# Last feed-forward stage: gate and up products of seventeen pairs as seven 256-column block products, with a hand-written order on every engine

## Chip, core and metric

The kernel runs on one core of a Trainium2 chip. The metric is the device time of one execution in microseconds (us), as the median over several runs. Matmuls run on TensorE (PE in the profile, its weight loads as PEld), elementwise work on VectorE (DVE) and ScalarE (ACT); GpSimd (POOL) and SyncE (SP) issue DMAs here.

## What is computed

A trunk of two layers on 512 tokens of width 1024 in float32. Each layer is half a feed-forward block, a mixer (Mamba-2 in layer 0, a diagonal state-space model "S5" in layer 1), and half a feed-forward block; an RMS norm ends the trunk.

```python
def rmsnorm(x, g):
    xf = x * lax.rsqrt(jnp.mean(x * x, axis=-1, keepdims=True) + NORM_EPS)
    return xf * g

def swiglu(h, w_in, w_out):                 # w_in 1024 x 5632, w_out 2816 x 1024
    gate, up = jnp.split(h @ w_in, 2, axis=-1)
    return (jax.nn.silu(gate) * up) @ w_out

for i in range(2):
    x = x + 0.5 * swiglu(rmsnorm(x, ffn1_norm[i]), ffn1_w_in[i], ffn1_w_out[i])
    x = x + mixer_i(rmsnorm(x, mix_norm[i]))
    x = x + 0.5 * swiglu(rmsnorm(x, ffn2_norm[i]), ffn2_w_in[i], ffn2_w_out[i])
return rmsnorm(x, final_norm)
```

## The kernel before

The residual stream stands transposed in SBUF as eight tiles `xT[d]` of 128 channels by 512 tokens. The stages run one after another: f1_0, ssd, f2_0, f1_1, s5, f2_1. The change concerns f2_1, the last, which ends in the final norm.

**Products in two parts.** Every matmul operand is split into a float32r value and a float32r remainder (`H` and `L` of the tokens, `hi` and `lo` of the weights). `proj` forms hi·H + hi·L + lo·H: three matmuls (lines 227, 228 and 229) for each 128-row slice of the contraction, each with its own 128x128 weight load and 512 moving columns. A weight tile goes through `fetch_w` (line 209, a DMA from the SP queue into `wst`), then `split_w`: a cast on ACT (line 218) and a subtraction on DVE (line 220).

**One feed-forward stage** (`ffn`). The 2816 hidden channels are 22 pairs: a gate tile and an up tile of 128 channels. A pair costs two projections of 24 matmuls each. Then DVE multiplies both by the norm's factor `rbc` (lines 259 and 262), ACT takes the silu (260), DVE multiplies (263), ACT casts (`ah`, 265) and DVE subtracts (`al`, 267). The pairs come in parts of 8, 7 and 7 (`PARTS`). After each part comes its share of the output projection: eight tiles `po`, each added to `xT[d]` by DVE (274). After the last part the new `xT[d]` goes to the final norm: ACT squares it (171) and scales it (`xg`, 1093), PE transposes it (1098), and DVE copies the result out (1099). `Prep.flush` issues the transposes of tile d when tile d+1 has been projected.

The norm's gain is multiplied into the tokens beforehand, but its factor `rbc` only reaches the result after the projection, so that the matmuls need not wait for the sum of squares. That sum is formed on PE (line 148) and `newton_rsqrt` on DVE, then spread by four transposes (157) and copied by ACT (204).

**What sets the order.** In this stage a scheduler orders all engines. In the trace each engine runs its instructions in the order in which they stand, so that one with an unmet wait holds all that stand behind it on its engine.

Of the kernel before, what the change touches and what calls it, by code (L numbers as in the profile page):

```python
# [9 lines left out]
F32 = mybir.dt.float32  # L10
F32R = mybir.dt.float32r
I32 = mybir.dt.int32
AF = mybir.ActivationFunctionType
OP = mybir.AluOpType
AX = mybir.AxisListType

T = 512
D = 1024
KD = 8
FF = 2816  # L20
FT = 22
# [4 lines left out]
MAN = {mybir.EngineType.PE}  # L26
# [4 lines left out]
def trunk_kernel(ctx, tc, x, ffn1_norm, ffn1_w_in, ffn1_w_out, mix_norm, ffn2_norm, ffn2_w_in, ffn2_w_out,  # L31
# [3 lines left out]
    nc = tc.nc  # L35
    V, S, G, PE = nc.vector, nc.scalar, nc.gpsimd, nc.tensor
# [3 lines left out]
    hpool = ctx.enter_context(tc.tile_pool(name="hpool", bufs=8))  # L40
    work = ctx.enter_context(tc.tile_pool(name="work", bufs=2))
# [3 lines left out]
    def mm_ps():  # L45
        return psum.tile([128, 512], F32, tag="mm", name="mm", bufs=4)

    def aux_ps():
        return psum.tile([128, 512], F32, tag="aux", name="aux", bufs=4)
# [23 lines left out]
    xT = [const.tile([128, T], F32, name=f"xT{d}") for d in range(KD)]  # L73
# [44 lines left out]
    def col(nm, j=0, n=1):  # L118
        i, r0 = C[nm]
        return cols[i][:, r0 + j:r0 + j + n]  # L120
# [32 lines left out]
    def bcast_rows(y4):  # L153

        p = aux_ps()
        for c in range(4):
            PE.transpose(p[:, c * 128:(c + 1) * 128], y4[:, c:c + 1].to_broadcast([128, 128]), ident)
        return p

    class Prep:  # L160


        def __init__(self, kind, gain, sink=None):
            self.kind, self.gain, self.sink = kind, gain, sink
            self.H, self.L = [None] * KD, [None] * KD
            self.acc = None
            self.later = []
# [25 lines left out]
        def sums(self):  # L193
            self.ps = compact_sum([self.acc, self.sq])
# [5 lines left out]
        def finish(self):  # L200
            self.y4 = newton_rsqrt(self.ps[:, 0:4], 4, 1.0 / D)
            if self.kind == "hilo":
                self.rbc = work.tile([128, T], F32, name="rbc")
                S.copy(self.rbc, bcast_rows(self.y4))


    def fetch_w(src, kt, eng=None):
        st = wpool.tile([128, KD, 128], F32, name="wst", bufs=4)[:, :kt]
        i = (eng or nc.sync).dma_start(st, src.rearrange("(k p) c -> p k c", p=128))
        return st, i  # L210

    def load_w(src, kt, eng=None):

        return split_w(fetch_w(src, kt, eng)[0], kt)

    def split_w(st, kt):
        hi = wpool.tile([128, KD, 128], F32R, name="whi", bufs=3)[:, :kt]
        S.copy(hi, st)  # L218
        lo = wpool.tile([128, KD, 128], F32R, name="wlo", bufs=3)[:, :kt]
        V.tensor_tensor(lo, st, hi.bitcast(F32), op=OP.subtract)  # L220
        return hi, lo

    def proj(ps, w, H, L, first=True, last=True):
        hi, lo = w
        n = len(H)
        for k in range(n):
            PE.matmul(ps, hi[:, k], H[k], start=first and k == 0, stop=False)  # L227
            PE.matmul(ps, hi[:, k], L[k], start=False, stop=False)  # L228
            PE.matmul(ps, lo[:, k], H[k], start=False, stop=last and k == n - 1)  # L229


    def ffn(pr, w_in, w_out, nxt, fill=(), ready=(), done=(), pad=0):

        fill, ready, done = list(fill), list(ready), list(done)

        def pop():
            if fill:
                fill.pop(0)()

        with tc.tile_pool(name="ffn", bufs=2) as fp:  # L240
            if pad:
                fp.tile([128, pad // 4], F32, name="pad", bufs=1)
            for a, b in PARTS:
                AH, AL = [], []
                for f in range(a, b):
                    if done:
                        pg, pu = done.pop(0)
                    else:
                        pg, pu = mm_ps(), mm_ps()
                        wg = ready.pop(0) if ready else load_w(w_in[:, f * 128:(f + 1) * 128], KD)  # L250
                        proj(pg, wg, pr.H, pr.L)
                        if f == 0:
                            pr.sums()
                        wu = ready.pop(0) if ready else load_w(w_in[:, FF + f * 128:FF + (f + 1) * 128], KD)
                        proj(pu, wu, pr.H, pr.L)
                        if f == 0:
                            pr.finish()
                    gt = fp.tile([128, T], F32, name="gt")
                    V.tensor_tensor(gt, pg, pr.rbc, op=OP.mult)  # L259
                    S.activation(gt, gt, AF.Silu)  # L260
                    up = fp.tile([128, T], F32, name="up")
                    V.tensor_tensor(up, pu, pr.rbc, op=OP.mult)  # L262
                    V.tensor_tensor(up, up, gt, op=OP.mult)  # L263
                    ah = fp.tile([128, T], F32R, name="ah", bufs=8)
                    S.copy(ah, up)  # L265
                    al = fp.tile([128, T], F32R, name="al", bufs=8)
                    V.tensor_tensor(al, up, ah.bitcast(F32), op=OP.subtract)  # L267
                    AH.append(ah)
                    AL.append(al)
                    pop()  # L270
                for d in range(KD):
                    po = mm_ps()
                    proj(po, load_w(w_out[a * 128:b * 128, d * 128:(d + 1) * 128], b - a), AH, AL)
                    V.scalar_tensor_tensor(xT[d], po, 0.5, xT[d], op0=OP.mult, op1=OP.add)  # L274
                    if b == FT:
                        nxt.flush()
                        nxt.take(d)
                    pop()
            while fill:
                fill.pop(0)()  # L280
        nxt.flush()
        if nxt.kind != "hilo":
            nxt.sums()
            nxt.finish()


    def ssd(pr, nxt):
# [295 lines left out]
    s5 = {}  # L583
# [503 lines left out]
    fin = {}  # L1087
# [17 lines left out]

    def prep_for(st):
        if st is None:
            fin["p"] = ctx.enter_context(tc.tile_pool(name="fin", bufs=2))
            return Prep("final", ("fin", 0), fin_sink)
        if st == "ssd":  # L1110
            return Prep("hilo", ("mix", 0))
        if st == "s5":
            s5["op"] = op_es.enter_context(tc.tile_pool(name="s5op", bufs=2))
            s5["up"] = up_es.enter_context(tc.tile_pool(name="s5u", bufs=2))
            return Prep("s5", ("mix", 8), s5_sink)
        L = int(st[-1])
        return Prep("hilo", (st[:2], 8 * L))
# [22 lines left out]
    with tc.manual_schedule(engines={mybir.EngineType.Activation, mybir.EngineType.DVE, mybir.EngineType.PE}):  # L1140
        xps, w = {}, {}
# [13 lines left out]
        def part(i, j, k, n=1):  # L1155
            proj(done[i][j], [w_[:, k:k + n] for w_ in w[2 * i + j]], prep.H[k:k + n], prep.L[k:k + n], first=k == 0,
                 last=k + n == KD)
# [52 lines left out]
    if "s5" in stages:  # L1210
        before = [s for s in stages[:stages.index("s5")] if s[0] == "f"]
        s5_pre = before[-3:-1]
    for i, s in enumerate(stages[:-1]):
        pr, prep = prep, prep_for(stages[i + 1])
        nxt = prep
        if s == "ssd":
            with tc.manual_schedule(engines=MAN):
                ssd(pr, nxt)
        elif s == "s5":
            with tc.manual_schedule(engines=MAN):  # L1220
                s5_stage(pr, nxt)
            op_es.close()
        else:
            L = int(s[-1])
            wi, wo = (ffn1_w_in, ffn1_w_out) if s[:2] == "f1" else (ffn2_w_in, ffn2_w_out)
            if s in s5_pre[:1]:
                ffn(pr, wi[L], wo[L], nxt, fill=pre0, ready=ready, done=done, pad=224)
                pre_es.close()
            elif s in s5_pre:
                with tc.tile_pool(name="pre1", bufs=2) as pp:  # L1230
                    ffn(pr, wi[L], wo[L], nxt, fill=s5_setup(pp, 1))
            elif stages[i + 1] == "s5":
                fill = [lambda: None] * 46
                for j in range(2):
                    for h in range(2):
                        fill[24 + 4 * h + 2 * j] = lambda j=j, h=h: out_ops(j, h)
                for j in range(2):
                    fill[40 + 2 * j] = lambda j=j: in_ops(j)
                fill[44] = lambda: out_ops(2, 0)
                for j in range(2 * NR):  # L1240
                    fill[39 + 2 * j] = lambda j=j: res_w(j)
                ffn(pr, wi[L], wo[L], nxt, fill=fill)
                up_es.close()
            else:
                ffn(pr, wi[L], wo[L], nxt)
    for t in range(4):
        if t % 2:
            V.tensor_scalar(fin["o"][:, t], fin["o"][:, t], prep.y4[:, t:t + 1], None, op0=OP.mult)
# [32 lines left out]
```

## Time and profile before

| | us |
|---|---|
| median of 3 runs (2090.33 to 2095.71) | 2092.37 |
| the profiled execution's own time | 2093.88 |
| its span | 2092.1 |
| last stage within the span: first matmul with its weights, end of the span | 1712.56, 2092.1 |
| PE busy, DVE busy, ACT busy over the span | 2035.6, 1250.0, 788.9 |

The span is the time that the profile covers; 1.8 us of the execution lie around it. All times in rows are counted from the span's start.

### The profile page before, as it was taken

Reading aid. Unit: us, or ns where it says so; the run is one execution under the profiler, and the core shown is the slowest. Engines: PE = TensorE matmul, PEld = TensorE weight load, DVE = VectorE, ACT = ScalarE, POOL = GpSimd, SP = SyncE. Lnnn points to the kernel's source line nnn. Section 1 sums busy time; section 2 is a strip of 40 time slices with the busy share of each in tenths; the row PEclk is TensorE's granted clock in tenths of the full one; section 3 lists DMA queues with packets and bytes.
Section 4 is the critical chain, followed back from the end, with each engine's and each line's share of the span. In section 5 each row is a group of like instructions: output and inputs, shape, how many; then the busy total and the mean of one; then the engine's idle time right before and its main releaser. Section 6 shows DMA issues by size and latency. Waiting matters only on the chain.

```text
span 2092.1 us, 26974 instructions
## 1 busy us (share of the span) xinstructions
PE 2035.6 (97%) x10675; PEld 1677.9 (80%) x10675; DVE 1250.0 (60%) x2119; ACT 788.9 (38%) x1140; POOL 84.6 (4%) x144
## 2 busy tenths in 40 slices
PE   8999999999999999999999999999996999999997
PEld 6788888878878877887788888888886888888886
DVE  6699445678875777557854554343458545444444
ACT  5223323556653574333423332232354333222223
POOL 1000000021110110000000000000011000000000
PEclk9999999999999999999999999999997999999999
DMA  7654432433333324435553353333367233333321
GB/s 163 136 160 142 148 100 83 111 116 105 101 108 114 107 64 125 144 113 162 145 145 89 102 193 91 102 94 104 91 191 235 62 90 101 101 94 88 110 84 58
DMA packets 411519, 244.29 MB, mean 117 GB/s; under 512 B 44952, under 2 KB 396864, under 8 KB 411136
## 3 DMA queue, kind: packets, MB, share of 16 engines
q1 hardware_dynamic: 381968, 203.19, 34.5%
q0 software_dynamic: 7984, 25.46, 3.7%
q10 hardware_dynamic: 21440, 13.91, 2.3%
q8 instruction: 84, 1.38, 0.3%
q14 instruction: 43, 0.35, 0.1%
HBM read 217.74 MB, written 24.25 MB: 116 GB/s over the span
## 4 chain that ended last, share of the span: by engine, by line
PE 59%; DVE 2%; ACT 1%; issue 1%; DVEq 0%; ACTq 0%
PE mm L227 19%; PE mm L228 19%; PE mm L229 19%; DVE z L1001 0%; PE aux L229 0%; PE aux L228 0%; PE aux L227 0%; PE aux L861 0%; PE aux L1019 0%; PE aux L867 0%; PE aux L992 0%; DVE z L997 0%; DVE z L999 0%; DVE z L998 0%; ACT z L1006 0%
## 5 line engine op out<-in xcount | busy, mean ns | idle before, releaser
L218 ACT CAST whi<-wst 128x1024 fp32r<-128x1024 f32 (+2 forms) x357 | 361.3, 1013 | 945.2 <-PE mm L228 662.8
L227 PE MATMUL mm<-hH,whi 128*128 128x512 f32 x1800 | 708.7, 394 | 5.8 <-ACT whi L218 4.1
L228 PE MATMUL mm<-hL,whi 128*128 128x512 f32 x1800 | 704.1, 391 | 0.0
L229 PE MATMUL mm<-hH,wlo 128*128 128x512 f32 x1800 | 703.2, 391 | 0.5 <-DVE wlo L220 0.5
L220 DVE TENSOR_TENSOR wlo<-wst,whi 128x1024 fp32r<-128x1024 f32 (+2 forms) x357 | 418.4, 1173 | 86.7 <-ACT whi L218 83.4
L227 PEld LDWEIGHTS mm<-hH,whi 128*128 128x128 f32 x1800 | 339.3, 189 | 77.6 <-ACT whi L218 4.5
L229 PEld LDWEIGHTS mm<-hH,wlo 128*128 128x128 f32 x1800 | 339.1, 188 | 72.6 <-DVE wlo L220 1.0
L228 PEld LDWEIGHTS mm<-hL,whi 128*128 128x128 f32 x1800 | 339.3, 189 | 69.6 <-issue 0.6
L228 PE MATMUL mm<-al,whi 128*128 128x512 f32 x704 | 274.5, 390 | 0.0
L229 PE MATMUL mm<-ah,wlo 128*128 128x512 f32 x704 | 274.2, 390 | 0.0
L227 PE MATMUL mm<-ah,whi 128*128 128x512 f32 x704 | 273.5, 390 | 0.0
L262 DVE TENSOR_TENSOR up<-mm,rbc 128x512 f32<-128x512 f32 x88 | 60.7, 690 | 213.4 <-PE mm L229 213.3
L274 DVE SCALAR_TENSOR_TENSOR xT<-mm,xT 128x512 f32<-128x512 f32 x96 | 66.0, 689 | 188.4 <-PE mm L229 188.3
L228 PEld LDWEIGHTS mm<-al,whi 128*128 128x128 f32 x704 | 132.2, 188 | 28.0 <-issue 0.6
L227 PEld LDWEIGHTS mm<-ah,whi 128*128 128x128 f32 x704 | 132.2, 188 | 27.5 <-issue 0.4
L229 PEld LDWEIGHTS mm<-ah,wlo 128*128 128x128 f32 x704 | 132.2, 188 | 27.3 <-issue 0.2
L259 DVE TENSOR_TENSOR gt<-mm,rbc 128x512 f32<-128x512 f32 x88 | 60.6, 689 | 149.7 <-PE mm L229 146.4
L384 DVE SCALAR_TENSOR_TENSOR cv<-raw,cols,cv 128x512 f32<-128x512 f32 x96 | 76.1, 803 | 7.0 <-ACT cv L382 6.4
L265 ACT CAST ah<-up 128x512 fp32r<-128x512 f32 x88 | 54.9, 624 | 65.7 <-DVE up L263 65.2
L263 DVE TENSOR_TENSOR up<-up,gt 128x512 f32<-128x512 f32 x88 | 60.7, 690 | 7.1 <-ACT whi L218 0.5
L267 DVE TENSOR_TENSOR al<-up,ah 128x512 fp32r<-128x512 f32 x88 | 60.0, 683 | 0.8 <-ACT ah L265 0.7
L260 ACT ACTIVATE gt<-gt 128x512 f32<-128x512 f32 x88 | 55.0, 627 | 13.7 <-DVE gt L259 8.5
(325 smaller groups left out, 1704.2 us busy)
## 6 DMA issues: line engine op xcount, KB each, us to landing
wst<-in_ffn_w_in_dram SPq DMA_DIRECT2D x176, 512.0 KB, 3.9
wst<-in_ffn_w_out_dram SPq DMA_DIRECT2D x64, 448.0 KB, 3.7
wst<-in_ssd_in_proj_dram SPq DMA_DIRECT2D x48, 512.0 KB, 4.0
wst<-in_ffn_w_out_dram SPq DMA_DIRECT2D x32, 512.0 KB, 4.0
dec<-d_cs POOLq DMA_DIRECT2D x16, 512.0 KB, 4.2
opP<-d_P SPq DMA_DIRECT2D x16, 512.0 KB, 5.4
wst<-in_s_glu_w_dram POOLq DMA_DIRECT2D x12, 512.0 KB, 5.3
d_t<-p_cs POOLq DMA_DIRECT2D x8, 512.0 KB, 4.2
```

The source lines that it names most:

```text
L218: S.copy(hi, st)
L220: V.tensor_tensor(lo, st, hi.bitcast(F32), op=OP.subtract)
L227: PE.matmul(ps, hi[:, k], H[k], start=first and k == 0, stop=False)
L228: PE.matmul(ps, hi[:, k], L[k], start=False, stop=False)
L229: PE.matmul(ps, lo[:, k], H[k], start=False, stop=last and k == n - 1)
L259: V.tensor_tensor(gt, pg, pr.rbc, op=OP.mult)
L260: S.activation(gt, gt, AF.Silu)
L262: V.tensor_tensor(up, pu, pr.rbc, op=OP.mult)
L263: V.tensor_tensor(up, up, gt, op=OP.mult)
L267: V.tensor_tensor(al, up, ah.bitcast(F32), op=OP.subtract)
L274: V.scalar_tensor_tensor(xT[d], po, 0.5, xT[d], op0=OP.mult, op1=OP.add)
L384: V.scalar_tensor_tensor(cv, raw[:, 1 + j:T + 1 + j], col("cw", j * 32 + ct), cv, op0=OP.mult, op1=OP.add)
```

## The change

`ffn7` takes the place of `ffn` in the last stage. Pairs 0 to 4 are computed as before. Meanwhile `build` forms the tokens after the norm (gain and `rbc` multiplied in) for the pairs 5 to 21.

For those, a pair is seen as a product of 2x2 blocks: gate and up tile, two halves of the contraction, two halves of 256 tokens. Seven block products, each of four 128-row slices, take the place of eight. `mul` issues one: 12 matmuls of 256 columns (lines 368 to 370). A pair has 84 of these where it had 48 of 512 columns. The sums that such a scheme needs are made in three places:

- of tokens, once: `build` makes seven blocks (`th` and `tl`, four slices each) from `n` and `t`;
- of weights, per pair: with `g` and `u` the gate and the up weights in two halves, `five` is u0+u1 (DVE, into PSUM), `six` is five+g0 (DVE), `add7` is u0+g0 and `add3` is six+g1 (both by an accumulating DMA from the POOL queue, 256 KB). `four` splits each of them on ACT (line 395) and DVE (398);
- of results: a product is accumulated in PSUM tiles `A`, `B` and `E`, and copied out (ACT lines 440, 480 and 499) between products that go on accumulating in `A`.

`iteration` writes the order of all engines down by hand. While PE works on pair `P`, DVE and ACT prepare the weights of the next, `N`, and finish the one before, `prev`. The seven products stand on PE in this order: W1 and (for `prev`) W3, W2, (for `prev`) W4, then W6, W7, W5. The pairs now come in parts of 5, 4, 4, 4 and 5. In a part with a `prev` left over, the first three tiles of the output projection are computed without its last pair and completed afterwards (`part`).

```diff
@@ class Prep, finish
-                self.rbc = work.tile([128, T], F32, name="rbc")
+                self.rbc = work.tile([128, T], F32, name="rbc", bufs=1)
@@ after ffn
+    def accumulate(dst, src):
+        G.dma_start(dst, src, accum_op=OP.add)
...
+    def ffn7(pr, w_in, w_out, nxt, parts, fill=(), late=None):
...
+        sv = es7.enter_context(tc.tile_pool(name="seven", bufs=2, side="right"))
...
+        def build(k):
...
+            def parts_of_u():
+                n = st["n"] = sv.tile([128, 4, 256], F32, tag="ut", name="tn", bufs=4)
+                for i, c in ((1, c0), (0, c1)):
+                    V.scalar_tensor_tensor(n[:, i], xT[k][:, c], g0, pr.rbc[:, c], op0=OP.mult, op1=OP.mult)
...
+            def sums():
+                n, t = st["n"], st["t"]
+                V.tensor_tensor(t[:, 3], n[:, 3], n[:, 0], op=OP.subtract)
+                V.scalar_tensor_tensor(t[:, 2], t[:, 1], -1.0, n[:, 3], op0=OP.mult, op1=OP.subtract)
+                V.scalar_tensor_tensor(t[:, 0], t[:, 2], -1.0, n[:, 2], op0=OP.mult, op1=OP.subtract)
+            def halves(j0, j1, src):
...
+                S.copy(TH[k][:, j0:j1], src)
+                V.tensor_tensor(TL[k][:, j0:j1], src, TH[k][:, j0:j1].bitcast(F32), op=OP.subtract)
+            return [parts_of_u, parts_of_v, sums, lambda: halves(0, 4, st["t"]), lambda: halves(4, 7, st["n"][:, 1:4])]
+        def mul(ps, w, j, first=False):
+            hi, lo = w
+            for k in range(4):
+                mh, ml = TH[k][:, j], TL[k][:, j]
+                PE.matmul(ps[:, c0], hi[:, k], mh, start=first and k == 0, stop=False, skip_group_check=True)
+                PE.matmul(ps[:, c0], hi[:, k], ml, start=False, stop=False, skip_group_check=True)
+                PE.matmul(ps[:, c0], lo[:, k], mh, start=False, stop=k == 3, skip_group_check=True)
...
+            def four(self, j, src, pool=None):
+                hi = hpool.tile([128, 4, 128], F32R, tag="hH", name="hH") if pool is None else \
+                    pool.tile([128, 4, 128], F32R, name="mh")
+                S.copy(hi, src)
...
+                V.tensor_tensor(lo, src, hi.bitcast(F32), op=OP.subtract)
+                self.W[j] = hi, lo
...
+        def iteration(i, prev, more, out):
...
+            mul(P.A, P.W[1], 4, first=True)
+            if prev:
+                prev.acc_u4()
+            if N:
+                N.five()
+                N.add7()
+            if prev:
+                prev.c22()
+            split(j + 1)
+            if N:
+                N.s12()
+                N.s5()
+            S.copy(P.gt[:, c0], P.A[:, c0])
+            if prev:
+                mul(prev.A, prev.W[3], 6)
+            if N:
+                N.s4()
+                N.six()
+            if prev:
+                prev.silu0()
+                prev.silu1()
+            P.s3()
+            mul(P.B, P.W[2], 5, first=True)
+            V.tensor_tensor(P.gt[:, c0], P.gt[:, c0], P.B[:, c0], op=OP.add)
+            if prev:
+                mul(prev.E, prev.W[4], 0)
+                prev.c21()
+            mul(P.A, P.W[6], 2)
+            if N:
+                N.s6()
+                N.add3()
+            S.copy(P.up[:, c0], P.A[:, c0])
+            if prev:
+                gated(prev.up, -1.0, prev.gt, out)
+            P.E = aux_ps()
+            mul(P.E, P.W[7], 3, first=True)
+            if N:
+                N.s7()
+            else:
+                split(j + 2)
+            mul(P.A, P.W[5], 1)
...
+                    if prev and d == 2:
+                        part(2, 0, n - 1)
+                        for e in range(3):
+                            part(e, n - 1, n)
+                        for e in range(3):
+                            split(j + 1 + e)
+                            fetch_to(j + 4 + e)
+                            after(e)
+                        continue
...
@@ the call in the last stage
-                ffn(pr, wi[L], wo[L], nxt)
+                    ffn7(pr, wi[L], wo[L], nxt, ((0, 5), (5, 9), (9, 13), (13, 17), (17, 22)), late=late)
```

`s4` calls `four` with the pool `sv`, whose tiles `mh` and `ml` have two buffers; the other splits use `hH` and `hL` with eight. The pool of the final norm's tiles is opened later than before (`late`).

**ACT, a pair in the middle of a part.** Before, the engine holds four kinds of rows per pair: two weight casts, the silu and the cast of the gated product.

```order
L218 CAST whi<-wst 128x1024
L260 ACTIVATE gt<-gt 128x512
L218 CAST whi<-wst 128x1024
L265 CAST ah<-up 128x512
L218 CAST whi<-wst 128x1024
```

Now one iteration (from the copy of `prev`'s up part to the split of W7) reads:

```order
L440 COPY up<-mm 128x256
L218 CAST whi<-wst 128x1024
L395 CAST hH<-aux 128x512
L480 COPY gt<-mm 128x256
L395 CAST mh<-wu 128x512
L446 ACTIVATE gt<-gt 128x256
L449 ACTIVATE gt<-mm 128x256
L395 CAST hH<-wu 128x512 x2
L499 COPY up<-mm 128x256
L376 CAST ah<-up 128x512
L395 CAST hH<-wu 128x512
```

`mh` is the cast of W4 for the next pair; the two casts after the silus are W3 of this pair and W6 of the next. The copy of line 499, for which PE's last product of the iteration waits, has moved behind all of them.

**DVE, pairs 0 to 4.** Before, between two gated products stood the rows of the pair and its two weight splits:

```order
L259 TENSOR_TENSOR gt<-mm,rbc 128x512
L220 TENSOR_TENSOR wlo<-wst,whi 128x1024
L262 TENSOR_TENSOR up<-mm,rbc 128x512
L263 TENSOR_TENSOR up<-up,gt 128x512
L220 TENSOR_TENSOR wlo<-wst,whi 128x1024
L267 TENSOR_TENSOR al<-up,ah 128x512
```

Now, from pair 2's gated product to pair 3's:

```order
L374 SCALAR_TENSOR_TENSOR up<-up,gt 128x512
L378 TENSOR_TENSOR al<-up,ah 128x512
L220 TENSOR_TENSOR wlo<-wst,whi 128x1024
L360 TENSOR_TENSOR tl<-tt,th 128x1024
L360 TENSOR_TENSOR tl<-tn,th 128x768
L534 TENSOR_TENSOR gt<-mm,rbc 128x512
L220 TENSOR_TENSOR wlo<-wst,whi 128x1024
L340 SCALAR_TENSOR_TENSOR tn<-xT_84,cols_101,rbc 128x256 x2
L345 SCALAR_TENSOR_TENSOR tn<-xT_88,cols_101,rbc 128x512
L347 TENSOR_TENSOR tt<-tn 128x256
L548 TENSOR_TENSOR up<-mm,rbc 128x512
```

`tn`, `tt`, `th` and `tl` are the token blocks of `build`: five rows of it stand between the pair's own.

**PE, end of the stage.** Before, the four transposes of one output tile stand between the matmuls of the next tile:

```order
L227 MATMUL mm<-ah,whi 128x512
L228 MATMUL mm<-al,whi 128x512
L1098 MATMUL aux<-ident,xg 128x128 x4
L229 MATMUL mm<-ah,wlo 128x512
L227 MATMUL mm<-ah,whi 128x512
```

Now the transposes of the first two tiles stand in one row, behind the three short completions and ahead of the fourth tile:

```order
L227 MATMUL mm<-ah,whi 128x512
L228 MATMUL mm<-al,whi 128x512
L229 MATMUL mm<-ah,wlo 128x512
L1434 MATMUL aux<-ident,xg 128x128 x8
L227 MATMUL mm<-ah,whi 128x512
```

The first two tiles have lost the matmuls that stood between their transposes.

More of the change, by code (lines that the diff above doesn't have):

```diff
@@ L1107, in prep_for @@
         if st is None:
-            fin["p"] = ctx.enter_context(tc.tile_pool(name="fin", bufs=2))
             return Prep("final", ("fin", 0), fin_sink)
@@ L1244, in trunk_kernel, with late @@
             else:
-                ffn(pr, wi[L], wo[L], nxt)
+                def late():
+                    fin["p"] = ctx.enter_context(tc.tile_pool(name="fin", bufs=2, side="right"))
+                with tc.manual_schedule(engines=MAN):
+                    ffn7(pr, wi[L], wo[L], nxt, ((0, 5), (5, 9), (9, 13), (13, 17), (17, 22)), late=late)
     for t in range(4):
```

208 lines of the change are left out of this document (added).

## Prediction

> **What bounds the kernel now.** I read the page first: the busy lines and the slices.
>
> ```profile
> span 2092.1 us, 26974 instructions
> PE 2035.6 (97%) x10675; PEld 1677.9 (80%) x10675; DVE 1250.0 (60%) x2119; ACT 788.9 (38%) x1140; POOL 84.6 (4%) x144
> ```
>
> PE is busy 97% of the span. Next the last stage alone, in windows (PE, PEld, DVE, ACT and POOL busy, clock, DMA share, GB/s), and PE's waits from 1734 us on.
>
> ```profile
> 1734.00:2050.00 316.00, 316.00 (x1396) 261.64 (x1395) 140.44 (x167) 90.12 (x109) 0.00 (x0) 1.00 0.33 95
> 2050.00:2076.50 26.50, 26.50 (x130) 21.96 (x129) 13.52 (x19) 9.07 (x13) 0.00 (x0) 1.00 0.00 1
> 2076.50:2092.10 15.60, 2.20 (x75) 1.57 (x73) 5.40 (x18) 3.43 (x4) 0.00 (x0) 0.68 0.34 136
> PE aux L1098 <- ACT xg L1093: 1.7, 1, 1.7
> ```
>
> PE runs without a hole at the full granted clock (1.00) until 2076.5 and waits once, 1.7 us. DVE works 140 of 316 us, ACT 90: all of it is hidden. So the stage is worth its matmuls, and everything else costs nothing as long as PE never waits. The timeline gives a matmul's price (start, duration, engine, line), ten in a row:
>
> ```profile
> 1799.92 0.39 PE L227 MATMUL mm<-hH,whi 128*128 128x512 f32 x1
> ...
> 1801.96 0.39 PE L227 MATMUL mm<-ah,whi 128*128 128x512 f32 x1
> ```
>
> Nine steps in 2.04 us are 0.2267 us each; the 0.39 is its life, so a result lands 0.39 - 0.227 = 0.16 us after PE has gone on.
>
> **Fewer matmuls.** A pair loses 48 x 0.2267 = 10.88 us and gains 84 products of 256 columns. No 256-column float32r matmul is in this trace. Nearest are float32 passes of the mixer stage, two per matmul (first the groups with a mean life, then the timeline):
>
> ```profile
> L461 PE MATMUL aux<-wx,btok 128*128 128x256 f32 x48 | 11.6, 378 | 0.0
> L431 PE MATMUL aux<-CT,BT 128*128 128x128 f32 x64 | 8.4, 274 | 0.0
> 438.80 1.46 PE L461 MATMUL aux<-wx,btok 128*128 128x256 f32 x6
> 431.23 1.05 PE L431 MATMUL aux<-CT,BT 128*128 128x128 f32 x8
> 431.01 1.08 PEld L431 LDWEIGHTS aux<-CT,BT 128*128 128x128 f32 x8
> ```
>
> Eight passes of 128 columns take (1.05 - 0.274)/7 = 0.111 us each, every one with its own full 128x128 load. So a load does not cost more than 0.111 us in a stream: that is the lower end. Six of 256 columns take (1.46 - 0.378)/5 = 0.216 each: the upper end, if float32r should run at that rate. I take half of 0.2267, 0.1133, since the 512-column steps are the same kind of matmul; it lies beside the lower end. A part of the 0.2267 may be fixed per matmul: if all that it has above L461's 0.216 is, 0.011, a 256-column product costs 0.119 (an estimate).
>
> The Trainium skill, "TensorE: Matmul & The Clock Gate", section "The mechanism", says that a weight load overlaps running matmuls only when the row groups differ, which full 128-row loads never do; by it each product would pay for its load as well. Taken with L431's 0.111 for the load, that would be 0.224 per product, 18.8 us a pair, and 135 us lost in place of 23 won. The trace disagrees: L431's loads and passes advance in the same 0.111 us.
>
> At 0.1133 a pair costs 84 x 0.1133 = 9.52, saves 1.36, and 17 pairs save **23.1 us**. The output projection stays at 528 matmuls.
>
> **What PE now waits for.** Rows for the walk (mean ns of one after the busy time), then the hand-over from ACT to DVE, and two DVE rows in succession:
>
> ```profile
> L220 DVE TENSOR_TENSOR wlo<-wst,whi 128x1024 fp32r<-128x1024 f32 x46 | 56.2, 1222 | 5.7 <-ACT whi L218 5.7
> L263 DVE TENSOR_TENSOR up<-up,gt 128x512 f32<-128x512 f32 x22 | 15.2, 692 | 2.5 <-ACT whi L218 0.5
> L218 ACT CAST whi<-wst 128x1024 fp32r<-128x1024 f32 x46 | 48.5, 1054 | 165.3 <-PE mm L228 107.3 <-issue 57.9
> L265 ACT CAST ah<-up 128x512 fp32r<-128x512 f32 x22 | 13.7, 624 | 13.9 <-DVE up L263 13.8
> L1093 ACT ACTIVATE xg<-xT,cols 128x512 f32<-128x512 f32 x8 | 5.7, 708 | 0.0
> L171 ACT ACTIVATE sq<-xT 128x512 f32<-128x512 f32 x8 | 5.0, 630 | 12.1 <-DVE xT L274 12.0
> 1722.94 1.05 ACT L218 CAST whi<-wst 128x1024 fp32r<-128x1024 f32 x1 [4.92 <-issue]
> 1724.02 1.22 DVE L220 TENSOR_TENSOR wlo<-wst,whi 128x1024 fp32r<-128x1024 f32 x1
> 1734.35 0.69 DVE L259 TENSOR_TENSOR gt<-mm,rbc 128x512 f32<-128x512 f32 x1 [1.25 <-ACT rbc L204]
> 1734.95 0.68 DVE L262 TENSOR_TENSOR up<-mm,rbc 128x512 f32<-128x512 f32 x1
> ```
>
> A hand-over takes 0.03 us; independent rows overlap by 0.1. Between the 512 and 1024 forms, 256 elements come to 0.41 us on ACT and 0.42 on DVE, 640 to 0.73 and 0.82 (estimates).
>
> *Middle of a part* (a pair with `prev` and `N`: 2 + 2 + 2 + 3 = 9 times). The `mh` tiles have two buffers, so ACT's cast of the next W4 waits until PE has used `prev`'s W4. Everything behind it on ACT waits too, up to the copy (L499) that the seventh product needs. From PE's last W4 matmul: landing 0.16, cast 0.66, DVE `ml` 0.72, `six` 0.72, ACT cast of W6 0.65, copy 0.31 (0.41 less the overlap), hand-over 0.03: 3.25 us. PE has W6 and W7 meanwhile, 24 x 0.1133 = 2.72. It waits 0.5. A stopped PE also starts with an unprefetched load:
>
> ```profile
> 919.27 0.50 PE L227 MATMUL mm<-ah,whi 128*128 128x512 f32 x1
> 919.61 0.39 PE L228 MATMUL mm<-al,whi 128*128 128x512 f32 x1
> 919.84 0.40 PE L229 MATMUL mm<-ah,wlo 128*128 128x512 f32 x1
> ```
>
> The first step is 0.34 instead of 0.23: 0.11 more per stop. ACT then still owes `ah`, W7's cast and the copy of `A` (L440) before W3 can go on: a second stop of 0.1 + 0.11. In all 0.8 x 9 = **7.2 us**.
>
> *Edges of parts.* A first iteration has no `prev` and only five products, 6.8 us, in which `add7` must land before W7's cast, which stands ahead of the copy L440: by the same walk small stops, 0.2 to 0.6 in three parts and 1.7 in the last: **3 us**.
>
> *Pairs 0 to 4.* From one gated product to the next the walk over the fenced order is: product 0.69, `ah` 0.62, `al` 0.68, split 1.22, `tl` 1.22 and 0.96, `gt` 0.69, silu 0.63, cast 1.05, split 1.22, `tn` 0.42 + 0.42 + 0.69, `tt` 0.42, `up` 0.69: 11.6, less eight overlaps, plus ten hand-overs: 11.1 us. PE's pair is 10.9. The chain starts at `rbc` (some 12.5 us into the stage, with a table load and the gated product: 15.8), needs 12 to 13 for the second pair and 11.1 to 11.2 for three more: about 62. PE has done five pairs and the first 12 matmuls of the projection at 5 x 10.88 + 0.9 + 2.7 = 58. It waits 4: with the load and `al`, **4.5 us**.
>
> *End of the stage.* The first two sets of transposes have no matmuls ahead of them. Between them stand ACT's cast 0.73, DVE's split 0.82, `xT` 0.59, square 0.63, `xg` 0.6 to 0.7, some 3.4 us, of which PE fills 0.6: waits of 1.9 (a part of the chain lies beside the completions) and 2.7. **4.8 us.**
>
> *Hidden.* DVE's rows per pair (nine of 512, three of 256, one of 1024 elements) come to 8.7 us, ACT's (six, five, one) to 6.8, both under 9.5. The weight DMAs move the same bytes. The accumulating DMAs have no row; the nearest are POOL's (KB, us to landing):
>
> ```profile
> wst<-in_s_glu_w_dram POOLq DMA_DIRECT2D x12, 512.0 KB, 5.3
> d_PR<-p_PR POOLq DMA_DIRECT2D x1, 288.0 KB, 4.0
> d_EI<-p_rEI POOLq DMA_DIRECT2D x1, 256.0 KB, 2.3
> ```
>
> I take 4, between 2.3 and 5.3, and none of it shows. In a first iteration `add7` has 6.8 + 1.36 - 0.7 (`five`) - 0.62 - 0.41 = 6.4 us until PE's next stop. `add3` of a middle pair is issued 4.0 us after one W4 product and needed 1.2 after the next, 10.3 later: 7.5 us.
>
> **The sum.** -23.1 + 7.2 + 3 + 4.5 + 4.8 = -3.6 us. The profiled execution took 2093.88 (span 2092.1 and 1.8 around it), 1.5 above the median of 2092.37; with the change 2090.3 against it, 2088.8 against the median. I take **2089 us**. About 0.3%, 6.3 us, is what a measurement can tell from no change.
>
> **The rivals.**
>
> *The waits are half of what I walked* (0.30). For it: the hand-overs are small differences of long sums; if the cast of W4 finds ACT and DVE a little faster, 0.5 us is gone nine times, and if pairs 0 to 4 keep up, 4.5 more. Against it: both chains consist of measured rows. The transposes stay. -23.1 + 4.8 + half of 14.7 = -11: 2081, from 2074 to 2086.
>
> *The 256-column product is dearer* (0.15). At 0.119, 84 x 17 x 0.0057 = 8.1 more, a third of which the waits absorb, as PE's cover grows: +5, so 2094. At 0.127, 19.6 more, it is +13: 2102. At L461's 0.216 it would be 17 x (18.1 - 10.9) = +122, 2214; 0.02 of the 0.15, because the 512-column rows contradict that rate. A load that isn't hidden, as by the skill's rule, belongs with this 0.02.
>
> *The accumulating DMA becomes the bound* (0.13, **slower**). Place: `add7` and `add3` on POOL's queue; W7's and W3's casts wait for them on ACT, and behind these the copies that PE needs. It decides from a landing of 6.4 us. At 9 us four first iterations lose 2.6 each and nine middle ones 1.5 each, 24 us, of which 7 replace waits already counted: -3.6 + 17 = +13, 2106. For it: an accumulation also has to read what it adds to, and the 512 KB transfers take 5.3. Against it: 256 KB rows take 2.3 to 4.0.
>
> The Trainium skill, "SBUF — State Buffer", section "SBUF: two separate sides", says that DMAs issued from GpSimd stand still while VectorE holds the port pair that both share; by it landings would lengthen with DVE's load, the more as DVE is busy most of the time here. No row shows such a block.
>
> **How the numbers follow.** My walk has 0.42, with a range of its own from 2084 to 2096. Faster than 2086.1: the first rival's 0.30 and 0.06 of the walk, 0.36. Slower than 2098.7: 0.08 of the second and all 0.13 of the third, 0.21. Same: 0.43. The range runs from 2076 to 2103; outside lie 0.05 of the first rival, 0.03 of the second and 0.11 of the third.
>
> **What the profile would show.** Matmuls of lines 368 to 370 start 0.113 us apart; PE's waits list ACT L499 (some 0.5 us, nine times), ACT L376 once with 4 us, and ACT L1429 with about 6.4 in all, 1.7 of it as before. The POOL DMAs land within 6 us. I am wrong if the steps are over 0.118, if PE waits for L395 behind a DMA, or if the waits for L499 don't appear.

## The result and the profile after

| | before | after |
|---|---|---|
| median of 4 runs each, us | 2091.35 (2089.16 to 2095.71) | 2103.3 (2102.79 to 2107.25) |
| the profiled execution | 2093.88 | 2103.28 |
| its span | 2092.1 | 2101.2 |
| last stage, first matmul to PE's last instruction | 367.7 | 376.1 |

The ratio is 1.0058, with a 95% interval from 1.0042 to 1.0074: the changed kernel is slower by 9 to 15 us. The forecast was 2089, some 3 us faster than before, with a range from 2076 to 2103. The time moved the other way and lies just above the range. The stage itself is 8.4 us longer.

First the head of the page of the changed kernel, as in the first fence of the prediction.

```profile
span 2101.2 us, 28700 instructions
PE 2029.2 (97%) x11287; PEld 1698.5 (81%) x11287; DVE 1330.5 (63%) x2306; ACT 841.8 (40%) x1300; POOL 113.2 (5%) x178
```

PE's busy time fell by 6.4 us and the span grew by 9.1: the change did take work off PE, and 15.5 us of idle time came instead. The same stretches as before (PE, PEld, DVE, ACT and POOL busy, clock, DMA share, GB/s) show where:

```profile
1734.00:2050.00 316.00, 306.41 (x1989) 279.73 (x1988) 211.77 (x340) 137.18 (x258) 28.77 (x34) 0.99 0.50 123
2050.00:2076.50 26.50, 21.79 (x108) 18.12 (x107) 13.31 (x21) 9.35 (x16) 0.00 (x0) 0.94 0.09 25
2076.50:2101.20 24.70, 11.73 (x120) 9.46 (x119) 10.77 (x26) 7.00 (x10) 0.00 (x0) 0.82 0.22 86
```

Before, PE was busy for 316.00 of the 316; now it is idle for 9.6 of them and for 4.7 of the next 26.5, and the granted clock is no longer 1.00. The price of a 256-column product stands in the timeline of a stretch without waits: 23 steps from the first row to the last.

```profile
1804.74 0.28 PE L369 MATMUL mm<-tl,whi 128*128 128x256 f32 x1
...
1807.50 0.28 PE L368 MATMUL mm<-th,hH 128*128 128x256 f32 x1
```

They take 2.76 us, 0.120 each. Seventeen pairs of 84 such products cost 171.4 us where 48 of 0.2267 cost 185.0: 13.6 us are saved, not 23.1. Next what PE waited for in the last stage, by its matmuls, then the stops at line 499 by its weight loads (us in total, times, longest):

```profile
PE aux L1434 <- ACT xg L1429: 6.4, 3, 2.7
PE mm L227 <- ACT ah L376: 4.9, 1, 4.9
PE mm L368 <- ACT up L440: 3.6, 3, 2.5
PE mm L228 <- DVE hL L186: 0.3, 1, 0.3
```

```profile
PEld mm L368 <- ACT up L499: 2.9, 9, 0.3
```

Every wait that the prediction named is there, at the row that it named. One cost was not named. After the one long wait PE goes on at half speed (timeline of PE, the idle time and its releaser in brackets):

```profile
1778.18 0.68 PE L227 MATMUL mm<-ah,whi 128*128 128x512 f32 x1 [4.94 <-ACT ah L376]
...
1779.92 0.63 PE L227 MATMUL mm<-ah,whi 128*128 128x512 f32 x1
1780.35 0.63 PE L228 MATMUL mm<-al,whi 128*128 128x512 f32 x1
```

The steps are 0.43 us there in place of 0.2267. With the starts of PE's instructions one behind the other, the stage's account closes:

| in the last stage, us | predicted | measured |
|---|---|---|
| 17 pairs, products | -23.1 | -13.6 |
| pairs 0 to 4: wait 5.1, late load and `al` 0.9 | +4.5 | +6.0 |
| half clock behind that wait | - | +1.0 |
| middle of parts: nine stops of 0.25 to 0.30 and 0.10 each, then 0.06 to 0.10 at the next copy | +7.2 | +4.2 |
| edges of parts: 0.99, 2.62, 0.45 and 0.10 each | +3 | +4.4 |
| first two sets of transposes | +4.8 | +4.9 |
| half clock behind them | - | +1.1 |
| sum | -3.6 | +8.0 (the stage: +8.4) |

At the edges ACT stood behind a DMA. This is ACT's timeline at the second iteration of part 4 (parts counted from one), then the DMA issues between 1930 and 1943 us, and last the same transfer in the page (KB each, median us to landing):

```profile
1936.88 0.36 ACT L499 COPY up<-mm 128x256 f32<-128x256 f32 x1
1942.07 0.62 ACT L395 CAST hH<-wu 128x512 fp32r<-128x512 f32 x1 [4.83 <-DMA wu<-wst]
1942.59 0.37 ACT L440 COPY up<-mm 128x256 f32<-128x256 f32 x1
```

```profile
wu<-in_ffn_w_in_dram SPq DMA_DIRECT2D x3, 512.0 KB, 8.9
wu<-wst POOLq DMA_DIRECT2D x2, 256.0 KB, 7.7
```

```profile
wu<-wst POOLq DMA_DIRECT2D x34, 256.0 KB, 4.2
```

The 34 accumulating DMAs land after 4.2 us, as taken. At this edge three weight transfers of 512 KB run at the same time. The two accumulating DMAs issued there land after 7.7 us in the median, and the one that ACT's cast waits for, issued at 1933.87, after 8.2. At the first iterations of parts 2 to 5 this landing took 3.2, 6.9, 8.2 and 6.3 us, and PE's stop was 0, 0.99, 2.62 and 0.45.

### The profile page after: what moved, and what is told of

It reads as the page before. It is cut to its first block, busy times and chain, and to the rows that moved or that the text cites. A ratio compares the mean times of both kernels' runs of the same rounds, so it can differ in the third digit from the quotient of the medians.

```text
span 2101.2 us, 28700 instructions
## 1 busy us (share of the span) xinstructions
PE 2029.2 (97%) x11287; PEld 1698.5 (81%) x11287; DVE 1330.5 (63%) x2306; ACT 841.8 (40%) x1300; POOL 113.2 (5%) x178
## 4 chain that ended last, share of the span: by engine, by line
PE 54%; DVE 4%; ACT 2%; issue 1%; DMA 1%; ACTq 0%; DVEq 0%
PE mm L227 15%; PE mm L228 15%; PE mm L229 15%; PE mm L368 2%; PE mm L370 1%; PE mm L369 1%; DMA wu<-wst 1%; DVE wlo L220 1%; ACT whi L218 1%; PE aux L369 1%; PE aux L368 1%; PE aux L370 0%; DVE z L1337 0%; PE aux L229 0%; PE aux L227 0%
## 5 line engine op out<-in xcount | busy, mean ns | idle before, releaser
L218 ACT CAST whi<-wst 128x1024 fp32r<-128x1024 f32 (+3 forms) x356 | 346.1, 973 | 754.5 <-PE mm L228 523.3
L227 PE MATMUL mm<-hH,whi 128*128 128x512 f32 x1528 | 603.1, 395 | 7.8 <-ACT whi L218 6.0
L228 PE MATMUL mm<-hL,whi 128*128 128x512 f32 x1528 | 598.2, 391 | 0.3 <-DVE hL L186 0.3
L229 PE MATMUL mm<-hH,wlo 128*128 128x512 f32 x1528 | 597.3, 391 | 0.0
L220 DVE TENSOR_TENSOR wlo<-wst,whi 128x1024 fp32r<-128x1024 f32 (+3 forms) x356 | 400.4, 1125 | 100.9 <-ACT whi L218 98.1
L229 PEld LDWEIGHTS mm<-hH,wlo 128*128 128x128 f32 x1528 | 288.0, 189 | 61.9 <-DVE wlo L220 0.8
L228 PEld LDWEIGHTS mm<-hL,whi 128*128 128x128 f32 x1528 | 288.2, 189 | 59.4 <-DVE hL L186 0.6
L368 PE MATMUL mm<-th,hH 128*128 128x256 f32 x204 | 59.7, 293 | 4.6 <-ACT up L440 3.6
L370 PE MATMUL mm<-th,hL 128*128 128x256 f32 x204 | 57.7, 283 | 0.0
L369 PE MATMUL mm<-tl,hH 128*128 128x256 f32 x204 | 57.7, 283 | 0.0
```

The source lines that it names most:

```text
L368: PE.matmul(ps[:, c0], hi[:, k], mh, start=first and k == 0, stop=False, skip_group_check=True)
L369: PE.matmul(ps[:, c0], hi[:, k], ml, start=False, stop=False, skip_group_check=True)
L370: PE.matmul(ps[:, c0], lo[:, k], mh, start=False, stop=k == 3, skip_group_check=True)
```

## The experiments

The theory after the result, **A**: the saving is 13.6 us because a float32r matmul has a fixed part, and four kinds of waits with the half clock behind them give 21.6 back. Its rivals: the price of 0.120 belongs to the surroundings of the products, the accumulating DMA is what binds, or the waits only move when one is removed. "Before" in each run is the kernel before, run on the same chip (medians 2093.5 to 2093.8 us, 10 to 21 runs), and "the changed kernel" is the 2103.3 of the result. The runs of an experiment and those of the changed kernel have only the kernel before in common, so the ratio to it stands beside each difference. Beside the changed kernel the kernel before read 2091.35, some 2 us less than beside the experiments; by the ratios each gain over the changed kernel is therefore 1 to 3 us larger than the plain difference.

**1. Halves, without the rest of the change.** The kernel before, with `proj` cutting the columns in the gate and up projections of pairs 5 to 21.

```diff
+            cs = [slice(c, c + cols) for c in range(0, T, cols)]
+            for c in cs:
+                PE.matmul(ps[:, c], hi[:, k], H[k][:, c], start=first and k == 0, stop=False, skip_group_check=True)
+            for c in cs:
+                PE.matmul(ps[:, c], hi[:, k], L[k][:, c], start=False, stop=False, skip_group_check=True)
```

> The kernel before with the projections of pairs 5 to 21 of the last stage issued in halves: 1632 matmuls of 256 columns in place of 816 of 512, nothing else. Theory A (a float32r matmul has a fixed part of 0.0133 us beside 0.2133 per 512 columns): steps of 0.120, 816 x (0.240 - 0.2267) = 10.9 us slower than before, about 2102. Theory B (the 0.120 of the changed kernel comes from what surrounds its products, and 256 columns alone cost half of 512): steps of 0.1133, no change, 2091. Theory C (a step cannot be shorter than the load of its 128x128 weights, some 0.12): like A here; the next kernel tells them apart.

> The same with quarters: 3264 matmuls of 128 columns. Theory A: steps of 0.0533 + 0.0133 = 0.0667, 816 x (0.2667 - 0.2267) = 33 us slower than before, 2124. Theory B: 0.0567, no change. Theory C: steps stay at 0.12, 816 x (0.48 - 0.2267) = 207 us slower, 2298 (with the 0.111 of the mixer's float32 passes 178 slower).

In both, each piece sets its own start flag, and the first slice's product hi·H is lost in all pieces but the last; the matmuls that run are all there. Measured: halves 2105.27, ratio 1.0057 [1.0043, 1.0071], 11.5 us slower; quarters 2274.8, ratio 1.0867 [1.0847, 1.0887], 181 us slower. In the timelines of the halves and of the quarters, 16 products lie between the starts of the two rows shown:

```profile
1800.07 0.40 PE L230 MATMUL mm<-hH,whi 128*128 128x256 f32 x2
...
1801.99 0.28 PE L234 MATMUL mm<-hH,wlo 128*128 128x256 f32 x1
```

```profile
1799.99 0.61 PE L234 MATMUL mm<-hH,wlo 128*128 128x128 f32 x4
...
1801.77 0.50 PE L230 MATMUL mm<-hH,whi 128*128 128x128 f32 x3
```

The halves take 1.92/16 = 0.120 in a kernel that has nothing of the change: theory B falls, and the stage is 10.9 us longer, as worked out. The quarters take 1.78/16 = 0.111, neither A's 0.0667 nor B's 0.0567. So there is a floor of 0.111, the same that the mixer's float32 passes of 128 columns showed; theory C had 178 us for it, against the 181 measured, and A can hold only above it. The three steps can be written as the larger of 0.111 and a fixed 0.0133 plus 0.2133 per 512 columns. With three constants for three widths this describes the steps and does not test the form: whether the excess at 256 columns is a fixed part or a weight load that shows through is not told apart. The price of 0.120 itself is shown.

**2. Pairs 0 to 4 with a lighter chain.** In the second half of each of the pairs 1 to 4 stands one block step less; these four steps move into the output projection.

```diff
-                        for _ in range(2):
-                            todo and todo.pop(0)()
+                        todo and todo.pop(0)()
                     V.tensor_tensor(up, pu, pr.rbc, op=OP.mult)
```

> The changed kernel with three steps of the token blocks per pair in pairs 1 to 4 where it had four; the rest of them goes into the output projection of the first part. Theory A (DVE and ACT fall behind in pairs 0 to 4, and PE pays 5.1 us of idle time, 0.9 after it and 1.3 at a halved clock): that wait is gone, 6 to 7 us faster than the changed kernel, about 2096.5. Rival: the steps only move, and PE stops as long at the first products of pair 5 or in the first projection: 2103.

Measured: 2097.56, ratio 1.0015 [1.0005, 1.0024], 5.7 us less than the changed kernel. PE's waits in the last stage:

```profile
PE aux L1433 <- ACT xg L1428: 6.4, 3, 2.7
PE mm L368 <- ACT up L440: 5.3, 3, 2.1
PE mm L228 <- DVE hL L186: 0.3, 1, 0.3
```

The wait for L376 is gone and none took its place. The timeline shows why: from one gated product (L374) to the next DVE takes 10.6, 10.5, 10.9 and 9.7 us, where the changed kernel has 12.9, 11.5, 11.5 and 11.3 and PE's pair takes 10.9. The profiled execution is the longest of the 11, 2101.12, and its stage is only 2.2 us shorter than the changed kernel's: the edges cost 1.7 more, the clock stayed halved for 6.8 us behind the transposes in place of 3.4, and it halved behind an edge too, where the steps go from 0.12 to 0.21.

```profile
1937.22 0.38 PE L368 MATMUL mm<-th,hH 128*128 128x256 f32 x1 [2.12 <-ACT up L440]
...
1939.22 0.41 PE L369 MATMUL mm<-tl,whi 128*128 128x256 f32 x1
1939.43 0.41 PE L370 MATMUL mm<-th,wlo 128*128 128x256 f32 x1
```

**3. Transposes later.** Each tile's transposes stand two or three tiles behind its `xg`; the final norm's pool has four buffers where it had two.

```diff
-                        nxt.flush()
+                        for _ in range((0, 0, 0, 1, 1, 2, 1, 1)[d]):
+                            nxt.later.pop(0)()
                         nxt.take(d)
```

> The changed kernel with the final norm's transposes of a tile issued two or three tiles later. Theory A (PE waits 2.2 and 2.7 us for the first two sets, and 1.1 more at a halved clock after them): 5 to 6 us faster than the changed kernel, about 2097.5. Rival (the chain of ACT and DVE per tile is as long as PE's 3.4 us, so that the wait moves to later sets): 2101 to 2103.

Measured: 2096.81, ratio 1.0012 [1.0003, 1.0021], 6.5 us less than the changed kernel; the stage is 370.7 us, 5.4 shorter. Its waits for transposes:

```profile
PE aux L1435 <- ACT xg L1430: 1.6, 2, 1.4
```

The two waits of 4.9 us are gone, the half clock behind them too, and what is left is the end of the stage that was there before. The rival falls: with matmuls of the next tiles ahead of them, the transposes find their tile ready.

**4. The edges: one sum per part on DVE.** `add7` of a part's second pair becomes a DVE addition.

```diff
-                N.add7()
+                N.add7(dve=prev is None)
...
+                if dve:
+                    V.tensor_tensor(self.u[:, 0:4], self.u[:, 0:4], self.g[:, 0:4], op=OP.add)
```

> The changed kernel; in the first pair of each of parts 2 to 5 the sum for W7 of the next pair is formed on DVE, not by the accumulating DMA (4 of the 34 sums). Theory A (at the edges of parts the accumulating DMA runs together with three weight transfers of 512 KB and lands late, ACT's cast of W7 waits for it, and PE stops for the copy behind that cast, 4.3 us in all): 2 to 4 us faster than the changed kernel, about 2100, and the stops at that copy are under 0.6 us each. Rival (what is late is the gate weights' own transfer): DVE then waits for it in place of the DMA queue, and holds all that stands behind on DVE: 2103 to 2108.

Measured: 2100.3, ratio 1.0038 [1.0026, 1.0051]. The stops at L440 are gone from PE's waits, and four short ones stand in their place (L502 is the copy that was L499):

```profile
PE mm L368 <- ACT up L502: 1.4, 4, 0.4
```

By PE's starts they are 0.51 and 0.10 each, 2.4 us in place of 4.4. The time agrees with a gain of 2 to 3 us, though its interval overlaps that of the changed kernel; the waits settle it. The stage is 1.2 us shorter and not 2.0, as the clock stayed halved for 6.8 us behind the transposes. At the edges DVE did not stand behind the gate weights: its four waits for them, 3.5 us in all, lie in the output projection, as they do in the changed kernel (4.0).

**5. The middle: W4 earlier.** On top of 4, PE's product of `prev` with W4 stands ahead of that with W3.

```diff
             if prev:
+                mul(prev.E, prev.W[4], 0)
                 mul(prev.A, prev.W[3], 6)
...
-                mul(prev.E, prev.W[4], 0)
                 prev.c21()
```

> As edge_dve, and the product with W4 of the pair before stands ahead of that with W3 and not behind W2, so that PE is done with W4 24 products earlier. Theory A (the nine stops in the middle of parts come from ACT's cast of the next W4, which waits for PE's use of the one before last): these stops vanish, 3.4 to 4.2 us faster than edge_dve, about 2096. Rival (ACT has too many rows there whatever the cast waits for): the stops stay or move to the product with W4, no change against edge_dve.

Measured: 2096.97, ratio 1.0014 [1.0005, 1.0023]; the stage is 371.0 us, 3.8 shorter than in 4. The stops in the middle are gone: PE's last stage has the four of L502 (again 1.4 in all), the long wait for L376 and the transposes, and no other at the seven products. So ACT's cast of the next W4, which waits for PE's use of the one before last, was the cause. In the changed kernel ACT's waits show it directly, nine times:

```profile
ACT mh L395 <- PE aux L369: 23.6, 9, 3.6
```

**6. All sums on DVE.** `accumulate` is replaced by a DVE addition at all 34 places.

```diff
-                accumulate(self.u[:, 4:8], self.g[:, 4:8])
+                V.tensor_tensor(self.u[:, 4:8], self.u[:, 4:8], self.g[:, 4:8], op=OP.add)
```

> The changed kernel with all 34 accumulating DMAs taken out: DVE forms add7 and add3 too, in the same places of the order. Theory A (the landing of 4.2 us is hidden except at the edges of parts; DVE's rows per pair go from 8.7 to 10.1 us, as long as PE's 10.1): edges gain 2 to 4, nine middle pairs get a second stop of 0.7 to 0.8, so 4 to 8 us slower than the changed kernel, 2107 to 2111. Rival (the accumulating DMA is the bound): 5 us or more faster than the changed kernel, 2098 or less.

Measured: 2107.3, ratio 1.0069 [1.0055, 1.0083], 4 us more than the changed kernel; the stage is 381.6 us, 5.6 longer. PE's waits at the seven products:

```profile
PE mm L368 <- ACT up L440: 5.0, 9, 0.6
...
PE mm L368 <- ACT up L499: 1.4, 4, 0.4
```

The edges gain as in 4, and nine second stops of 0.55 us (0.7 by PE's starts) appear in the middle. Without any accumulating DMA the kernel is slower, so that DMA is not what bounds it.

**7. The four edits together.** 2, 3, 4 and 5 in one kernel.

> Four edits together: three token-block steps per pair (chain), later transposes (lag), the early W4 product, and the four sums on DVE at the edges. Theory A (products of 0.120 us save 13.6 us, and waits of the four kinds gave back 22): with 3 to 5 us of waits left, 9 to 10 us faster than before, about 2083, ratio 0.995 to 0.996. Rival (the lost time is contention that a higher pace brings back, or the halved clock appears at other places): 2090 or more.

Measured: 2082.04, ratio 0.9944 [0.9931, 0.9958] to before: 9 to 14 us faster than before, 21 less than the changed kernel. The two stretches up to the last tile, and PE's waits:

```profile
1734.00:2050.00 316.00, 314.59 (x2057) 288.88 (x2056) 220.21 (x349) 142.65 (x265) 25.39 (x30) 1.00 0.48 121
2050.00:2068.00 18.00, 16.39 (x84) 13.22 (x83) 14.32 (x22) 10.27 (x17) 0.00 (x0) 1.00 0.01 1
```

```profile
PE aux L1437 <- ACT xg L1432: 1.6, 2, 1.4
PE mm L368 <- ACT up L502: 1.4, 4, 0.4
```

PE is idle for 1.4 of the 316 us, and the clock is 1.00 throughout. The stage is 356.9 us: 19.1 shorter than in the changed kernel, which is the 21.6 of the account less the 2.4 that still stand at L502. Against before it is 10.7 shorter, 13.6 of saved products less those 2.4, with 0.5 left over that is not assigned. No contention came up at the higher pace.

**8. One more copy moved.** In a part's first pair the copy of L499 stands ahead of the cast of W6.

```diff
+            if not prev:
+                S.copy(P.up[:, c0], P.A[:, c0])
             if N:
                 N.s6()
                 N.add3()
-            S.copy(P.up[:, c0], P.A[:, c0])
+            if prev:
+                S.copy(P.up[:, c0], P.A[:, c0])
```

> As all_waits; in the first pair of a part, which has no pair before it, ACT's copy of the up product stands ahead of the cast of the next W6. Theory A (all_waits has four stops of 0.51 us and a late load of 0.10 left there, 2.4 us): they go, 2 to 2.5 us faster than all_waits, ratio to before 0.993 to 0.994, about 2080. Rival (the cast of W6 comes so late that the next copy of ACT holds PE): no change, 0.9944.

Measured: 2081.59, ratio 0.9940 [0.9926, 0.9953]. In the trace the four stops are gone and the stage is 354.6 us, 2.3 shorter; in the time the step from 2082.04 is not resolved. Together with 7 it is the fastest of these kernels.

**9. Work in the hole.** The changed kernel, with 18 unused matmuls ahead of the last slice in the first projection.

```diff
+                        part(d, 0, n - 1)
+                        spare = mm_ps()
+                        for _ in range(18):
+                            PE.matmul(spare, h[:, 0], AH[0], start=True, stop=True)
```

> The changed kernel with 18 matmuls of 512 columns, whose result is not used, ahead of the last slice of pairs 0 to 4 in the first projection of the output: 4.1 us of work in the 5.1 us in which PE waits there. Theory A (the granted clock halves because PE stood idle): the remaining wait is about 1 us, and the steps behind it stay at 0.227 us in place of 0.427; the time is 1 us lower or the same within what can be measured. Rival (the halving comes at that time whatever PE does): steps of 0.427 remain behind the wait.

Measured: 2102.79 (3 runs), no different from the changed kernel, as A allowed. The stretch from 1778 to 1782 us in the changed kernel and in this one (the clock is the number after POOL):

```profile
1778.00:1782.00 4.00, 3.77 (x9) 2.69 (x10) 3.84 (x7) 1.97 (x4) 0.00 (x0) 0.57 0.23 70
```

```profile
1778.00:1782.00 4.00, 3.85 (x17) 3.15 (x18) 4.00 (x8) 1.32 (x3) 0.00 (x0) 1.00 0.29 82
```

With PE kept busy the clock stays at 1.00, and 17 matmuls fit where 9 did. The half clock follows from PE's idle time. It was worth 1.0 us at this place.

## Why the prediction was wrong

**The failing step is the price of a product**: "I take half of 0.2267, 0.1133, since the 512-column steps are the same kind of matmul". That they are the same kind does not make the price proportional. Halves in the old kernel show 0.120, so the term "17 pairs save 23.1 us" was 13.6, and the 9.5 us between them exceed the whole gain that was forecast. They are the largest part of the 11.6 us between the two sums of the account. The rows for it were in the prediction: it worked out 0.119 from the part of 0.2267 that stands above L461's 0.216, and then gave that a chance of 0.15 as a rival. The two bounds were 0.111 and 0.216; 0.1133 was chosen because it lay beside the lower one, while a fixed part can only move the half upward. The Trainium skill, "TensorE: Matmul & The Clock Gate", section "Back-to-back issue gap", gives N/2.4 ns plus about 2.5 for an isolated matmul: 0.216 for 512 columns and 0.109 for 256. These steps are 0.011 longer at both widths, so for float32r the page's fixed part is too small here, and the measurement decides. Its section "LDWEIGHTS (loading the stationary operand)" puts a load of 128 columns at 128/1.2, 0.107 us. The 0.111 floor of the quarters lies close to that; that the load makes the floor is an inference, which no run here isolates.

**The second rival was the right mechanism.** It held that dearer products leave PE more cover, and that the waits absorb a third of the extra. The stops in the middle came out at 4.2 in place of 7.2, 3.0 less, a third of 9.5. That it is just a third is partly luck: the added cover, 24 x 0.0067 = 0.16 us a stop, accounts for 1.4 us at the nine first stops, and the rest is not taken apart. Its price for 0.119 was 2094 and for 0.127 2102. By its rule 0.120 comes to 2095; the half clock, the chain and the edges below add 2.1, 1.5 and 1.4, which makes 2100.

**The half clock was not seen**: 2.1 us in the changed kernel, behind two waits that the prediction itself placed. The trace of before has a clock of 0.68 in its last stretch, where PE mostly waits; it was quoted, and not carried over to the new waits. Behind the transposes the half clock lasted 3.4 us in the profiled execution of the changed kernel and 6.8 in those of runs 2, 4, 5, 6 and 9, some 1 us dearer.

**The chain of pairs 0 to 4** was walked to 4.5 and cost 6.0. The direction and the place were right. The walk had 12 to 13 us for the second pair and 11.1 to 11.2 for three more; they took 12.9, 11.5, 11.5 and 11.3, so that each of the last three was 0.2 to 0.4 longer than walked.

**Edges of parts**: 3 predicted, 4.4 measured, and for a reason that belongs to the third rival. The accumulating DMA landed after 4.2 us on the whole, as taken, but after 6.3 to 8.2 at three of the four edges; that rival was to decide from 6.4. Its place was right, its size not: run 4 won back 2 us, not 17. In the middle of parts it bounds nothing: of ACT's six waits for it in the changed kernel three are at these edges and three in the output projection, where PE does not stop for them.

```profile
ACT hH L395 <- DMA wu<-wst: 14.2, 6, 4.8
```

That the weight transfers make it late is argued from the edges (at the first, where it landed after 3.2 us, two of the three had landed or were within 1 us of it, and the third was issued later) and not isolated by a run. DVE's load, the other reason that the prediction names, finds no support. Inside the longest landing DVE stood idle (the third busy time), while the DMA engines were full (share 1.13):

```profile
1938.76:1942.17 3.41, 1.80 (x15) 1.59 (x14) 0.00 (x0) 0.10 (x1) 0.23 (x1) 1.00 1.13 281
```

**The transposes** (4.8, measured 4.9) and the nine stops in number, place and cause were right; the stops were shorter than walked, 0.25 to 0.30 us in place of 0.5. It was also right to neglect DVE's and ACT's rows: with four orders mended the kernel keeps the clock at 1.00 and PE idle for 1.4 of 316 us.

**The first rival** had the waits at half of what was walked. In this stage they and the clock came to 21.6, a little over the 19.5 of the walk.

**The signs of being wrong** that the prediction named: the steps are over 0.118, and PE stopped behind a cast of L395 that waited for a DMA, at three edges. The third, missing waits for L499, did not come.

The 12 us between the medians stand against 9.4 between the two profiled executions and 8.4 in the stage; the interval of 9 to 15 holds the 9.4. The rest is about what the kernel before varied by: it read 2091.35 in the 4 runs of the result and 2093.5 to 2093.8 in the 10 to 21 runs beside each experiment, against which 2103.3 is 9.5 to 9.8 longer.

## What to carry to other kernels

Price an instruction of a new size by two measured sizes, a fixed part and a rate, and not by proportion, and look for a floor below them (128 columns took 0.111 us where that line gives 0.067): over 17 pairs of 84 products, 0.007 us each came to 9.5 us, more than the whole forecast gain of 3.6. When a change saves a little on the bounding engine by writing an order by hand, look for the places where that engine first waits for work that another engine finishes late. Here four small moves of rows, none of which removed any work, were worth 21 us and turned a slower kernel into a faster one. A saving on an engine that is busy 97% of the time is real only as long as nothing new makes it wait; the account in the stage, term by term from the starts of its instructions, says which term to mend.

## What the runs showed of the hardware

- A float32r matmul with its own 128x128 weights took 0.2267, 0.120 and 0.111 us at 512, 256 and 128 columns. Halving 512 columns costs 6%; quartering nearly doubles the cost per column.
- In this stage the granted clock fell to half behind waits of PE, for 3.4 or 6.8 us. It did so after a gap of 5.3 us between PE's starts and not when 18 matmuls filled it. It also did so after one of 2.4 us in run 2, and did not after one of 3.3 us in run 3, so the length of the gap alone does not decide. Where it lies does. In each trace all changes of the clock stand whole multiples of 3.413 us apart (in the changed kernel 1778.33, 1781.75, 2065.05 and 2068.47; the 283.30 in the middle are 83 of them). Cut into windows on that grid, the two gaps read, run 2 first (the clock is the number after POOL):

```profile
1935.03:1938.44 3.41, 1.29 (x11) 1.22 (x11) 1.51 (x3) 2.01 (x4) 0.00 (x0) 1.00 1.01 242
1938.44:1941.85 3.41, 3.41 (x19) 3.41 (x18) 1.85 (x3) 0.69 (x2) 0.84 (x1) 0.50 0.63 104
```

```profile
1936.26:1939.68 3.42, 1.91 (x16) 1.71 (x15) 0.00 (x0) 0.00 (x0) 0.35 (x1) 1.00 1.14 287
1939.68:1943.09 3.41, 1.90 (x16) 1.90 (x16) 2.19 (x4) 2.69 (x5) 0.59 (x1) 1.00 0.54 112
```

  In run 2 PE was idle for 2.12 us of one window, and the next ran at 0.50. In run 3 the longer gap fell half into each of two windows, 1.5 us idle in both, and the clock stayed at 1.00. Over the last stage of all twelve traces, up to the last tile's matmuls, every window at full clock with 2.10 us idle or more (twelve of them) was followed by a halved one, and none with 1.77 or less; between the two no trace has a window. The Trainium skill, "TensorE: Matmul & The Clock Gate", section "HAM oscillation — how this bites in real kernels", warns of idle gaps over about 3.4 us. The gap of 2.4 us shows that shorter ones can cost as well. The free-running window of 3.4 us, which the same page describes in "What's actually happening", agrees with the grid in these traces.
- An accumulating DMA of 256 KB from SBUF to SBUF landed after 4.2 us in the median of 34, after 3.2 at the soonest, and after 8.2 in the changed kernel beside three transfers of 512 KB.
